# A two-layer diffusion-transformer block on one core: transposes of the attention weights, the place of four modulation parts, and the order of the mLSTM stage

## The chip, the core and the metric

The kernel runs on one core of one Trainium2 chip. TensorE multiplies matrices, VectorE and ScalarE do element-wise work, GpSimd (POOL in the profile) does element-wise work and issues DMAs from its own queue, SyncE (SP) issues DMAs. The metric is the device time of one execution in microseconds, as the median of several runs.

## The reference

All tensors are float32; the model width is 1024, the sequence 1024, the context 256. Each layer takes six modulation vectors from the condition, then a mixer and a mixture of experts with their residuals:

```python
def adaln(cond, w, b):
    m = jax.nn.silu(cond) @ w + b
    return jnp.split(m[..., None, :], 6, axis=-1)

for layer in range(2):
    sh1, sc1, gt1, sh2, sc2, gt2 = adaln(c, w_mod[layer], b_mod[layer])
    hx = modulate(x, norm_mix_g[layer], sh1, sc1)
    if layer == 0:   # mLSTM heads and sliding-window attention, both over ctx too
        hc = modulate(ctx, norm_mix_g[0], csh1, csc1)
        yx, _ = mixer_ab(hx, hc, ...)     # concat(mLSTM, attention) @ w_out
    else:
        yx = mixer_chunk_gmlp(hx, ...)
    x = x + gt1 * yx
    x = x + gt2 * ec_moe(modulate(x, norm_ffn_g[layer], sh2, sc2), ...)
return rmsnorm(x, final_norm_g)
```

The window attention has eight heads of 64. A block of 128 queries sees up to three blocks of 128 keys and all 256 context keys, with a sink added to the softmax's denominator. The mLSTM has four heads of 128 that run over eight chunks forward and backward. In `ec_moe` each of 16 experts takes its 128 best tokens.

## The kernel before

Matrix products are made of three products of rounded halves: high by high, low by high, high by low. `split` makes the halves of a weight: the high one on ScalarE (line 70), the low one on VectorE or GpSimd (line 71). A list scheduler decides the order of the instructions on each engine from the program, so the program's order is a wish. The stages, by the time of the profile:

- **First stage, 0 to 93 us** (`start`, `start_mod`, `heads_context`). x and ctx are loaded (tiles xt), normed and transposed; the first two modulation parts are computed from eight 1 MB loads wm that SyncE issues; the context's keys and values of the four mLSTM heads are projected, and their transposes stored.
- **Projections, 93 to 156 us** (`layer0_a`): keys, values, gates of the latent sequence. Line 298 is the matmul of every projection.
- **Attention, 156 to 596 us** (`attention`). Four pairs of heads c by eight query blocks n: 32 turns, each with two heads i. Scores S go to PSUM (two buffers in `pss`), ScalarE makes P = exp(S - max) and its row sums, VectorE the reciprocal of the denominator, `den`. Then each 128x128 tile of P is multiplied by a diagonal matrix `dg` = identity x den: this transposes and scales it at once (line 492, 304 tiles). The result is split to PH and PL and multiplied by the values. `fill(n)` hands out other work between those steps, 4, 2 and 3 steps a turn: the next heads' queries and the projections of the mLSTM heads. With every 28 of its steps come nine of `mods`.
- **mods** are ten of the twelve modulation parts (layer, w), in `mod_part`: eight steps of a 512 KB load wm on GpSimd's queue (line 667; `lm` holds two) and four matmuls of the weights against the 32-column condition (line 670), then the bias, and two transposes into `modc` or, for w = 2 and 5, a write to `s_gt`.
- **mLSTM and output projection, 596 to 825 us** (`lstm_main`, `lstm_finish`, `out_w`, `out_tile`, `layer0_b`). For each head and direction d: nP is the log-decay matrix and gets a mask (line 726), aq is multiplied by qT (line 732), kt is k transposed (line 718), wk and wc are k weighted by the state factors (lines 730, 728). The first head's element-wise work of that kind is on VectorE, that of the others on GpSimd. `out_w` loads w_out in 512 KB pieces and splits them, low halves on GpSimd.
- **Routing of the first layer, 825 to 850 us** (`route`): the router's scores lg are transposed, sorted on VectorE by a network of small operations, and the chosen tokens are gathered.
- **Experts, 850 to 1440 us** (`experts`), gMLP to 2078, second routing and experts to 2718. Expert weights come as 1 MB tiles mraw from SyncE into a ring (`moe_tile`), some ahead of the routing; tiles whose index is in `HELD` are held back and issued on GpSimd after the gather.

What line 492 does stands in these lines:

```python
dg = hp.tile([128, 128], F32, tag="dg", name="dg", bufs=2)
nc.vector.tensor_scalar(dg, self.ident, den, None, op0=ALU.mult)
...
nc.tensor.matmul(S[i][:, ...], P[:, j * 128:(j + 1) * 128], dg, start=True, stop=True)
```

## Time and profile before

| | |
|---|---|
| median of 3 runs | 2725.24 us (2724.99 to 2725.42) |
| the profiled execution | 2720.4 us, of which the span from first to last instruction is 2718.6 us |
| mean granted clock of TensorE in it | 0.968 |
| busy: TensorE, VectorE, ScalarE, GpSimd | 2529.9, 1879.9, 1511.4, 626.0 us |
| DMA | 644.02 MB, mean 237 GB/s |

A busy share is a mean over stages with different limits, so the share of a stretch is read beside it. Matmuls are pipelined: the duration of one instruction contains time in which the next already runs, and the distance from one start to the next is its price.

### The profile page before, as it was taken

Reading aid. Unit: us, or ns where it says so; the run is one execution under the profiler, and the core shown is the slowest. Engines: PE = TensorE matmul, PEld = TensorE weight load, DVE = VectorE, ACT = ScalarE, POOL = GpSimd, SP = SyncE. Lnnn points to the kernel's source line nnn. Section 1 sums busy time; section 2 is a strip of 40 time slices with the busy share of each in tenths; the row PEclk is TensorE's granted clock in tenths of the full one; section 3 lists DMA queues with packets and bytes.
Section 4 is the critical chain, followed back from the end, with each engine's and each line's share of the span. In section 5 each row is a group of like instructions: output and inputs, shape, how many; then the busy total and the mean of one; then the engine's idle time right before and its main releaser. Section 6 shows DMA issues by size and latency. Waiting matters only on the chain.

```text
span 2718.6 us, 35149 instructions
## 1 busy us (share of the span) xinstructions
PE 2529.9 (93%) x12847; PEld 2005.4 (74%) x12847; DVE 1879.9 (69%) x2830; ACT 1511.4 (56%) x2258; POOL 626.0 (23%) x413
## 2 busy tenths in 40 slices
PE   5999999998895999999998999999995999999996
PEld 3767777777774788888776887888884788888774
DVE  5566656567737999999885184116505899999887
ACT  4344344334424888888775223232322888888774
POOL 0010111115421222221102434533451021231001
PEclk8999999999996999999999999999997999999998
DMA  7344554457166999999966323342335999999995
GB/s 261 103 128 141 152 160 142 144 185 265 48 238 234 352 388 380 387 380 386 374 215 202 101 67 119 117 147 70 101 108 190 376 373 388 380 381 382 359 363 186
DMA packets 241642, 644.02 MB, mean 237 GB/s; under 512 B 18609, under 2 KB 85341, under 8 KB 240445
## 3 DMA queue, kind: packets, MB, share of 16 engines
q1 hardware_dynamic: 205136, 530.52, 52.3%
q0 software_dynamic: 25840, 89.99, 11.7%
q10 hardware_dynamic: 10492, 21.26, 2.3%
q8 instruction: 101, 1.65, 0.2%
q14 instruction: 73, 0.59, 0.1%
HBM read 589.06 MB, written 50.02 MB: 235 GB/s over the span
## 4 chain that ended last, share of the span: by engine, by line
PE 80%; DVE 8%; DMA 4%; issue 4%; ACT 3%; POOL 1%; POOLq 0%; ACTq 0%; SPq 0%; DVEq 0%
PE g L1134 13%; PE u L1134 13%; PE d L1134 12%; PE acc L298 8%; PE acc L1444 7%; PE acc L1518 6%; PE acc L1466 6%; PE S L492 2%; PE acc L805 2%; PE acc L670 2%; DMA wm<-in_w_mod_dram 1%; PE tr L1164 1%; DVE s2k L1460 1%; PE tr L1208 1%; PE O L501 1%
## 5 line engine op out<-in xcount | busy, mean ns | idle before, releaser
L71 DVE TENSOR_TENSOR ml<-mraw,mh 128x1024 fp32r<-128x1024 f32 x750 | 875.3, 1222 | 61.7 <-ACT mh L70 61.2
L70 ACT ACTIVATE mh<-mraw 128x1024 fp32r<-128x1024 f32 x750 | 769.3, 1064 | 138.6 <-PE g L1134 67.8
L71 POOL TENSOR_TENSOR wl<-wraw,wh 128x1024 fp32r<-128x1024 f32 (+1 forms) x132 | 253.6, 1930 | 349.8 <-ACT wh L70 349.8
L70 ACT ACTIVATE wh<-wraw 128x1024 fp32r<-128x1024 f32 (+1 forms) x163 | 143.0, 893 | 311.0 <-issue 123.6
L1232 POOL DMA_INDIRECT s_x<-xe,idx x28 | 66.9, 2388 | 655.0 <-ACT hidH L1210 394.4
L1134 PE MATMUL g<-mh,xH 128*128 128x512 f32 x512 | 206.4, 403 | 1.4 <-ACT xH L1169 1.4
L1134 PE MATMUL g<-ml,xH 128*128 128x512 f32 x512 | 205.3, 401 | 1.5 <-DVE ml L71 1.4
L1134 PE MATMUL g<-mh,xL 128*128 128x512 f32 x512 | 204.4, 399 | 0.0
L1134 PE MATMUL u<-ml,xH 128*128 128x512 f32 x512 | 203.4, 397 | 0.2
L1134 PE MATMUL u<-mh,xL 128*128 128x512 f32 x512 | 202.2, 395 | 0.0
L1134 PE MATMUL u<-mh,xH 128*128 128x512 f32 x512 | 202.2, 395 | 0.0
L1134 PE MATMUL d<-ml,hidH 128*128 128x512 f32 x496 | 197.5, 398 | 5.0 <-DVE ml L71 4.9
L1152 POOL DMA_INDIRECT xe<-s_xr,idx x32 | 137.7, 4303 | 270.7 <-ACT mh L70 131.0
L1134 PE MATMUL d<-mh,hidH 128*128 128x512 f32 x496 | 198.2, 400 | 1.6 <-DVE o L1229 1.6
L1134 PE MATMUL d<-mh,hidL 128*128 128x512 f32 x496 | 196.3, 396 | 0.0
L1444 PE MATMUL acc<-wh,h2k 128*128 128x512 f32 x512 | 163.7, 400 | 1.8 <-DVE h2k L1426 1.7
L1466 PE MATMUL acc<-h2k,wh 128*128 128x512 f32 x512 | 161.5, 396 | 0.0
L298 PE MATMUL acc<-hH,wh 128*128 128x512 f32 (+1 forms) x368 | 155.4, 422 | 1.6 <-DVE mrows L676 0.5
L1518 PE MATMUL acc<-wh,s2k 128*128 128x512 f32 x480 | 152.1, 397 | 0.0
L298 PE MATMUL acc<-hL,wh 128*128 128x512 f32 (+1 forms) x368 | 145.7, 396 | 0.0
L298 PE MATMUL acc<-hH,wl 128*128 128x512 f32 (+1 forms) x368 | 145.7, 396 | 0.0
L667 POOL DMA_DIRECT2D wm<-in_w_mod_dram x80 | 42.7, 534 | 406.6 <-PE acc L670 382.1
(469 smaller groups left out, 5238.9 us busy)
## 6 DMA issues: line engine op xcount, KB each, us to landing
mraw<-in_moe_w_down_dram SPq DMA_DIRECT2D x128, 1024.0 KB
mraw<-in_moe_w_gate_dram SPq DMA_DIRECT2D x126, 1024.0 KB
mraw<-in_moe_w_up_dram SPq DMA_DIRECT2D x124, 1024.0 KB
wm<-in_w_mod_dram POOLq DMA_DIRECT2D x80, 512.0 KB, 4.2
wraw<-in_gm_w_in_dram SPq DMA_DIRECT2D x64, 512.0 KB
wraw<-in_gm_w_out_dram SPq DMA_DIRECT2D x32, 512.0 KB
wraw<-in_ab_w_in_dram SPq DMA_DIRECT2D x30, 512.0 KB
wm<-in_w_mod_dram SPq DMA_DIRECT2D x8, 1024.0 KB
```

The lines of the kernel that those rows point to most:

```text
L70: nc.scalar.activation(h, src, AF.Copy)
L71: i = (nc.gpsimd if eng == "pool" else nc.vector).tensor_tensor(l, src, h.bitcast(F32), op=ALU.subtract)
L298: nc.tensor.matmul(acc, a[:, k, :], b[:, k, c0:c0 + n], start=(k == 0 and i == 0), stop=(k == KD - 1 and i == 2))
L492: nc.tensor.matmul(S[i][:, 512 - nl + j * 128:640 - nl + j * 128], P[:, j * 128:(j + 1) * 128], dg, start=True, stop=True)
L670: nc.tensor.matmul(acc[32 * j:32 * j + 32, :], lhs, wm[:, 256 * j:256 * (j + 1)], start=(k == 0), stop=(k == KD - 1))
L805: nc.tensor.matmul(acc, a[:, k, t * 128:(t + 1) * 128], b[:, k % 2, :], start=(k == 0 and i == 0), stop=(k == 3 and i == 2))
L1134: nc.tensor.matmul(acc[:, sl], a[:, k, :], b[:, sl], start=(k == 0 and i == 0), stop=(k == KD - 1 and i == 2))
L1152: f = nc.gpsimd.indirect_dma_start(out=xe, out_offset=None, in_=self.s_xr[layer], in_offset=bass.IndirectOffsetOnAxis(ap=self.idx[e], axis=0))
L1232: nc.gpsimd.indirect_dma_start(out=self.s_x[layer], out_offset=bass.IndirectOffsetOnAxis(ap=self.idx[e], axis=0), in_=o, in_offset=None, c ...
L1444: nc.tensor.matmul(acc[t], a[k][:, ts], b[:, k2, :], start=(k == 0 and i == 0), stop=(k == KD - 1 and i == 2))
L1466: nc.tensor.matmul(acc, a[:, k, :], b[k], start=(k == 0 and i == 0), stop=(k == KD - 1 and i == 2))
L1518: nc.tensor.matmul(acc, a[:, ts], b[k2], start=(c == 0 and i == 0), stop=(c == 15 and i == 2))
```

## The change

- `attention`: no dg. VectorE multiplies P by den in place, the whole 640 or 512 columns at once, after the first `fill`; then every tile is transposed through the identity.
- Four modulation parts leave the attention. Parts (0,2) and (0,3) go into the first stage: their wm tiles use the buffers of x's tiles, their loads stay on GpSimd's queue, and their sixteen steps are handed out in `heads_context`. Parts (1,3) and (1,4), called `HOLE`, are loaded as eight 1 MB tiles by SyncE into the ring of expert weights ahead of the output projection, and multiplied in the first layer's `route`, after the transpose of the scores, with ScalarE and GpSimd for what follows. The attention keeps six parts, one step of them with every fifth `fill` step.
- `lstm_main`: the mask additions and the products aq x qT are written ahead of the transposes of k.
- `out_w`: the low halves are made on VectorE.
- `HELD` is given for each layer; the first layer's is (18, 23), where the eight tiles of `HOLE` count in the index, and five tiles are held; the second keeps (11, 14).

```diff
                         yield
-            self.heads_context(late, pt, Ws, rows())
-    def heads_context(self, s, pt, Ws, more):
+            pm = self.pool(late, "pmod0", space=PSUM)
+            mods = itertools.chain(*(self.mod_part(xp, "xt", sm, pm, pt, 0, w) for w in (2, 3)))
+            self.heads_context(late, pt, Ws, rows(), mods)
+    def heads_context(self, s, pt, Ws, more, mods):
         nc = self.nc
...
             list(itertools.islice(more, 2))
+            list(itertools.islice(mods, (1, 1, 3, 3)[hd]))
             W = Ws.pop(0) if Ws else self.w_in(1024 + hd * 128)
...
             list(itertools.islice(more, 2))
+            list(itertools.islice(mods, (0, 2, 3, 3)[hd]))
         store(*kept)
-        for _ in more:
+        for _ in itertools.chain(more, mods):
             pass
...
                 nc.vector.reciprocal(den, den)
-                dg = hp.tile([128, 128], F32, tag="dg", name="dg", bufs=2)
-                nc.vector.tensor_scalar(dg, self.ident, den, None, op0=ALU.mult)
-                Ps.append((P, dg))
+                Ps.append((P, den))
             fill(self.FILLS[0])
...
                     fill(self.FILLS[1])
-                P, dg = Ps[i]
+                P, den = Ps[i]
+                nc.vector.tensor_scalar(P[:, 0:w], P[:, 0:w], den, None, op0=ALU.mult)
                 for j in range(nt):
-                    nc.tensor.matmul(S[i][:, 512 - nl + j * 128:640 - nl + j * 128], P[:, j * 128:(j + 1) * 128], dg, start=True, stop=True)
+                    nc.tensor.transpose(S[i][:, 512 - nl + j * 128:640 - nl + j * 128], P[:, j * 128:(j + 1) * 128], self.ident)
                 src = S[i][:, row].rearrange("p (j q) -> p j q", q=128)
...
             Qs = [Q, [], [], []]
-            mods = itertools.chain(*(self.mod_part(lm, pa, pt, i // 6, i % 6) for i in range(2, 12)))
+            mods = itertools.chain(*(self.mod_part(lm, "wm", lm, pa, pt, i // 6, i % 6) for i in range(4, 12) if (i // 6, i % 6) not in self.HOLE))
             work = itertools.chain(*(itertools.chain(self.query(pa, qp, c + 1, hx, Qs[c + 1]) if c < 3 else (),
...
                 for _ in itertools.islice(work, n):
-                    i = next(steps)
-                    if 9 * (i + 1) // 28 > 9 * i // 28:
+                    if next(steps) % 5 == 4:
                         next(mods, None)
...
                                         kh[base:base + 64, c0:c0 + n].bitcast(F32), op=ALU.subtract)
-    def mod_part(self, pool, pa, pt, layer, w):
-        nc, I = self.nc, self.I
+    def mod_step(self, acc, k, wm):
+        for j in range(4):
+            self.nc.tensor.matmul(acc[32 * j:32 * j + 32, :], self.silw[:, k].rearrange("p a s -> p (a s)"), wm[:, 256 * j:256 * (j + 1)],
+                                  start=(k == 0), stop=(k == KD - 1))
+    def mod_bias(self, pool, layer, w, bufs=1):
+        b = self.I["b_mod"]
+        bias = pool.tile([128, 256], F32, tag="mbias", name="mbias", bufs=bufs)
+        self.nc.gpsimd.dma_start(out=bias, in_=bass.AP(tensor=b.tensor, offset=b.offset + 6 * D * layer + D * w, ap=[[256, 4], [0, 32], [1, 256]]))
+        return bias
+    def mod_columns(self, rows, pt, layer, w, copy):
+        tr = pt.tile([128, 512], F32, tag="tr", name="tr")
+        for t in range(2):
+            self.nc.tensor.transpose(tr[:, t * 128:(t + 1) * 128], rows[:, t * 128:(t + 1) * 128], self.ident)
+        copy(self.modc[:, layer, 8 * w:8 * w + 8].rearrange("p (j t) -> p j t", t=2),
+             tr[:, 0:256].rearrange("p (t j r) -> p j t r", t=2, j=4)[:, :, :, 0])
+    def mod_part(self, wp, tag, pool, pa, pt, layer, w):
+        nc = self.nc
         acc = pa.tile([128, 512], F32, tag="acc", name="acc")[:, 0:256]
         for k in range(KD):
-            wm = pool.tile([128, D], F32, tag="wm", name="wm")
-            nc.gpsimd.dma_start(out=wm, in_=I["w_mod"][layer, k * 128:(k + 1) * 128, D * w:D * (w + 1)])
-            lhs = self.silw[:, k].rearrange("p a s -> p (a s)")
-            for j in range(4):
-                nc.tensor.matmul(acc[32 * j:32 * j + 32, :], lhs, wm[:, 256 * j:256 * (j + 1)], start=(k == 0), stop=(k == KD - 1))
+            wm = wp.tile([128, D], F32, tag=tag, name="wm")
+            nc.gpsimd.dma_start(out=wm, in_=self.I["w_mod"][layer, k * 128:(k + 1) * 128, D * w:D * (w + 1)])
+            self.mod_step(acc, k, wm)
             yield
+        bias = self.mod_bias(pool, layer, w)
         rows = pool.tile([128, 256], F32, tag="mrows", name="mrows", bufs=1)
-        bias = pool.tile([128, 256], F32, tag="mbias", name="mbias", bufs=1)
-        b = I["b_mod"]
-        nc.gpsimd.dma_start(out=bias, in_=bass.AP(tensor=b.tensor, offset=b.offset + 6 * D * layer + D * w, ap=[[256, 4], [0, 32], [1, 256]]))
         nc.vector.tensor_tensor(rows, acc, bias, op=ALU.add)
...
         else:
-            tr = pt.tile([128, 512], F32, tag="tr", name="tr")
-            for t in range(2):
-                nc.tensor.transpose(tr[:, t * 128:(t + 1) * 128], rows[:, t * 128:(t + 1) * 128], self.ident)
-            nc.vector.tensor_copy(self.modc[:, layer, 8 * w:8 * w + 8].rearrange("p (j t) -> p j t", t=2),
-                                  tr[:, 0:256].rearrange("p (t j r) -> p j t r", t=2, j=4)[:, :, :, 0])
+            self.mod_columns(rows, pt, layer, w, nc.vector.tensor_copy)
         yield
+    HOLE = ((1, 3), (1, 4))
+    def hole_load(self):
+        self.hole = []
+        for layer, w in self.HOLE:
+            for kp in range(4):
+                raw = self.moe_tile()
+                self.nc.sync.dma_start(out=raw, in_=self.I["w_mod"][layer, 256 * kp:256 * (kp + 1), D * w:D * (w + 1)].rearrange("(k p) c -> p k c", p=128))
+                self.hole.append(raw)
+    def hole_mods(self, p, ps, pt):
+        for i, (layer, w) in enumerate(self.HOLE):
+            acc = ps.tile([128, 512], F32, tag="mod", name="mod")[:, 0:256]
+            for k in range(KD):
+                self.mod_step(acc, k, self.hole[4 * i + k // 2][:, k % 2, :])
+            rows = p.tile([128, 256], F32, tag="mrows", name="mrows", bufs=2)
+            self.nc.scalar.activation(rows, acc, AF.Copy)
+            self.mod_columns(rows, pt, layer, w, lambda o, x: self.nc.scalar.activation(o, x, AF.Copy))
+            m = self.modc[:, layer, 8 * w:8 * w + 8]
+            self.nc.gpsimd.tensor_tensor(m, m, self.bcols[:, 48 * layer + 8 * w:48 * layer + 8 * w + 8], op=ALU.add)
     def lstm_main(self, lp, hd):
...
         nc.sync.dma_start(out=og, in_=self.s_o[hd])
+        eng = nc.gpsimd if hd else nc.vector
+        for d in range(2):
+            mask = self.maskb if d else self.maskf
+            eng.tensor_tensor(nP[d], nP[d], mask[:, None, :].to_broadcast([128, NT, 128]), op=ALU.add)
+        for d in range(2):
+            nc.vector.tensor_tensor(aq[d], aq[d], qT, op=ALU.mult)
         kt = lp.tile([128, NT, 128], F32, tag="kt", name="kt")
...
             nc.tensor.matmul(S[:, c * 128:(c + 1) * 128], kT[:, c * 128:(c + 1) * 128], qT[:, c * 128:(c + 1) * 128], start=True, stop=True)
-        eng = nc.gpsimd if hd else nc.vector
         for d in range(2):
-            mask = self.maskb if d else self.maskf
-            eng.tensor_tensor(nP[d], nP[d], mask[:, None, :].to_broadcast([128, NT, 128]), op=ALU.add)
             wc.append(lp.tile([128, 2, 128], F32, tag="wc", name="wc", bufs=2))
...
         for d in range(2):
-            nc.vector.tensor_tensor(aq[d], aq[d], qT, op=ALU.mult)
             u = self.psn.tile([128, 130], F32, tag="num", name="num")
...
             Ws.append(self.load_w(self.I["ab_w_out"][0, r0:r0 + 256, 512 * cb:512 * (cb + 1)].rearrange("(k p) c -> p k c", p=128), [128, 2, 512],
-                                  dma=self.nc.gpsimd))
+                                  "dve", dma=self.nc.gpsimd))
         return Ws
...
             self.moe_open(self.m0, 0, 8)
+            self.hole_load()
             lp = self.pool(s, "lp2")
...
         tr = pp.tile([128, 512], F32, tag="tr", name="tr")
-        nc.tensor.transpose(tr[:, 0:128], lg.rearrange("p t e -> p (t e)"), self.ident)
+        last = nc.tensor.transpose(tr[:, 0:128], lg.rearrange("p t e -> p (t e)"), self.ident)
         rows = p.tile([128, 128], F32, tag="rows", name="rows")
...
                     nc.vector.match_replace(work[:, h:h + 64], s1[:, h + 8 * r:h + 8 * r + 8], work[:, h:h + 64], -1.0)
+        if layer == 0:
+            with self.tc.issue_after(last.ins):
+                self.hole_mods(p, self.hole_ps, self.hole_pt)
         def stages(src, dst, n, sizes):
...
     def moe_raw(self, name, layer, e, kp):
-        held = self.HELD[0] <= self.mrawi < self.HELD[1]
+        h0, h1 = self.HELD[layer]
+        held = h0 <= self.mrawi < h1
         raw = self.moe_tile()
...
         return raw
-    HELD = (11, 14)
+    HELD = ((18, 23), (11, 14))
     def moe_w(self, name, layer, e, k, low=True):
...
                 pp = self.pool(r, "rpp0", bufs=3, space=PSUM)
+                self.hole_ps = self.pool(r, "rmod", bufs=2, space=PSUM)
+                self.hole_pt = self.pool(r, "rmpt", bufs=2, space=PSUM)
                 self.route(rw, pp, 0)
```

VectorE in the attention, around the two heads of one turn; ast holds the maxima, sums and den, mx and PL belong to the turns before. Before:

```order
L477 TENSOR_TENSOR ast<-ast 128x1
L473 SCALAR_TENSOR_TENSOR ast<-ast,nsink 128x1
L478 RECIPROCAL ast<-ast 128x1
L480 TENSOR_SCALAR dg<-cst,ast 128x128
L508 TENSOR_TENSOR mx<-O,mx 64x256
L477 TENSOR_TENSOR ast<-ast 128x1
L478 RECIPROCAL ast<-ast 128x1
L480 TENSOR_SCALAR dg<-cst,ast 128x128
L495 TENSOR_TENSOR PL<-S,PH 128x5x128 x2
```

After:

```order
L481 TENSOR_TENSOR ast<-ast 128x1
L477 SCALAR_TENSOR_TENSOR ast<-ast,nsink 128x1
L482 RECIPROCAL ast<-ast 128x1
L493 TENSOR_SCALAR P<-P,ast 128x640
L71 TENSOR_TENSOR wl<-wraw,wh 128x1024
L481 TENSOR_TENSOR ast<-ast 128x1
L482 RECIPROCAL ast<-ast 128x1
L493 TENSOR_SCALAR P<-P,ast 128x640
L498 TENSOR_TENSOR PL<-S,PH 128x5x128 x2
```

The diagonal was made right behind the reciprocal; now the scaling of P stands there. In the rows of after, the low half of a weight (wl) stands between the two heads' chains.

TensorE in the first stage, around the last transposes of the context's keys and values (kcT, vcT); xt is x, cH and cL are the context's halves. Before:

```order
L228 MATMUL tr<-cst,kcT 128x128
L229 MATMUL tr<-cst,vcT 128x128
L228 MATMUL tr<-cst,kcT 128x128
L229 MATMUL tr<-cst,vcT 128x128
L213 MATMUL tr<-cst,xt 128x128 x8
L228 MATMUL tr<-cst,kcT 128x128
L229 MATMUL tr<-cst,vcT 128x128
L228 MATMUL tr<-cst,kcT 128x128
L229 MATMUL tr<-cst,vcT 128x128
L298 MATMUL acc<-cH,wh 128x256
L298 MATMUL acc<-cL,wh 128x256
L298 MATMUL acc<-cH,wl 128x256
```

After:

```order
L230 MATMUL tr<-cst,kcT 128x128
L231 MATMUL tr<-cst,vcT 128x128
L230 MATMUL tr<-cst,kcT 128x128
L231 MATMUL tr<-cst,vcT 128x128
L213 MATMUL tr<-cst,xt 128x128 x8
L665 MATMUL acc<-wm,silw 32x256 x16
L230 MATMUL tr<-cst,kcT 128x128
L231 MATMUL tr<-cst,vcT 128x128
L230 MATMUL tr<-cst,kcT 128x128
L231 MATMUL tr<-cst,vcT 128x128
L677 MATMUL tr<-cst,mrows 128x128 x2
L302 MATMUL acc<-cH,wh 128x256
```

Sixteen of the 64 matmuls L665 (four of the sixteen steps; in the profile each is two instructions) stand between the transposes of x and those of the last head, and the two transposes of a finished part ahead of the projections that follow; the other 48 stand further up.

GpSimd at the start of the mLSTM stage, with the halves and loads of w_out (wl, wraw) and the second head's nP and wc. Before:

```order
L71 TENSOR_TENSOR wl<-wraw,wh 128x1024 x2
L78 DMA wraw<-in_ab_w_out_dram 128x2x512 x2
L71 TENSOR_TENSOR wl<-wraw,wh 128x1024
L728 TENSOR_TENSOR wc<-kctx,colG 128x256 x2
L78 DMA wraw<-in_ab_w_out_dram 128x2x512
L726 TENSOR_TENSOR nP<-nP,cst 128x1024 x2
```

After:

```order
L78 DMA wraw<-in_ab_w_out_dram 128x2x512 x2
L767 TENSOR_TENSOR wc<-kctx,colG 128x256 x2
L753 TENSOR_TENSOR nP<-nP,cst 128x1024 x2
L78 DMA wraw<-in_ab_w_out_dram 128x2x512
L769 TENSOR_TENSOR wk<-kt,colG 128x1024
```

The low halves that stood ahead of the second head's wc and nP are no longer in GpSimd's queue.

## Rows read from the trace of the kernel before

**Rows 1.** The page, part 1: busy us and share of the span by engine.

```profile
PE 2529.9 (93%) x12847; PEld 2005.4 (74%) x12847; DVE 1879.9 (69%) x2830; ACT 1511.4 (56%) x2258; POOL 626.0 (23%) x413
```

**Rows 2.** Busy time by stretch: stretch, length, engines' busy us, granted clock, DMA share, GB/s.

```profile
20.00:50.00 30.00, 19.01 (x112) 11.28 (x112) 12.66 (x40) 12.88 (x26) 0.00 (x0) 0.77 1.01 349
50.00:100.00 50.00, 38.52 (x268) 35.20 (x269) 44.34 (x91) 31.20 (x55) 0.34 (x2) 0.86 0.39 109
200.00:600.00 400.00, 395.25 (x2583) 301.99 (x2582) 237.57 (x508) 156.35 (x326) 46.79 (x86) 1.00 0.49 153
600.00:750.00 150.00, 121.57 (x700) 103.71 (x699) 115.63 (x212) 73.94 (x251) 79.49 (x62) 0.91 0.45 161
830.00:843.00 13.00, 0.00 (x0) 0.00 (x0) 12.14 (x82) 5.85 (x7) 1.45 (x3) 0.50 0.56 205
900.00:1400.00 500.00, 497.37 (x2325) 400.72 (x2324) 467.93 (x476) 419.24 (x517) 98.92 (x26) 1.00 1.01 376
```

**Rows 3.** Timeline of TensorE: start, us, operation, count, idle time before and its releaser.

```profile
843.27 0.60 PE L1017 MATMUL tr<-sort,cst 32*16 32x128 f32 x2 [14.88 <-DVE sort L1003]
```

**Rows 4.** Groups of instructions by shape, TensorE, 156 to 600 us.

```profile
L492 PE MATMUL S<-dg,P 128*128 128x128 f32 x608 | 81.2, 280 | 2.3 <-DVE ast L477 1.7 <-DVE dg L480 0.6
L670 PE MATMUL acc<-wm,silw 128*32 128x256 f32 x624 | 56.6, 391 | 1.9 <-DMA wm<-in_w_mod_dram 1.8
```

**Rows 5.** Timeline of TensorE from 305 us.

```profile
305.48 0.40 PE L298 MATMUL acc<-hH,wl 128*128 128x512 f32 x1
305.80 0.64 PE L670 MATMUL acc<-wm,silw 128*32 128x256 f32 x8
306.37 0.50 PE L298 MATMUL acc<-hH,wh 128*128 128x512 f32 x1
306.71 0.40 PE L298 MATMUL acc<-hL,wh 128*128 128x512 f32 x1
306.94 0.39 PE L298 MATMUL acc<-hH,wl 128*128 128x512 f32 x1
...
309.20 1.38 PE L492 MATMUL S<-dg,P 128*128 128x128 f32 x10
310.34 0.48 PE L298 MATMUL acc<-hH,wh 128*128 128x512 f32 x1
```

**Rows 6.** Timeline of TensorE from 664 us, the transposes of kT.

```profile
664.30 0.60 PE L718 MATMUL tr<-cst,kT 128*128 128x128 f32 x4
664.74 1.28 PE L722 MATMUL S<-qT,kT 128*128 128x128 f32 x10
```

**Rows 7.** Groups of instructions by shape, VectorE, 156 to 600 us.

```profile
L71 DVE TENSOR_TENSOR wl<-wraw,wh 128x1024 fp32r<-128x1024 f32 x16 | 19.5, 1221 | 6.4 <-ACT wh L70 6.2
L480 DVE TENSOR_SCALAR dg<-cst,ast 128x128 f32<-128x128 f32 x64 | 18.1, 286 | 3.8 <-issue 2.3
...
L312 DVE TENSOR_SCALAR hx<-pad,convw 128x1024 f32<-128x1024 f32 x8 | 6.0, 753 | 0.0
```

**Rows 8.** The chain that ended last, first stage: start, us, what.

```profile
24.40 9.38 DMA wm<-in_w_mod_dram
```

**Rows 9.** One tile, wm, 156 to 600 us.

```profile
DMA to landing us min/median/max: 3.8/4.2/7.5
```

**Rows 10.** Groups of instructions by shape, GpSimd, 590 to 860 us.

```profile
L71 POOL TENSOR_TENSOR wl<-wraw,wh 128x1024 fp32r<-128x1024 f32 x8 | 19.4, 2428 | 22.1 <-ACT wh L70 22.1
```

**Rows 11.** The chain that ended last, mLSTM stage.

```profile
607.13 5.07 POOL wl L71 x2
...
776.65 2.40 POOL wl L71
```

**Rows 12.** Groups of instructions by shape, VectorE, 590 to 800 us.

```profile
L732 DVE TENSOR_TENSOR aq<-aq,qT 128x1024 f32<-128x1024 f32 x8 | 13.4, 1697 | 0.0
```

**Rows 13.** Timeline of VectorE from 305 us.

```profile
307.30 0.16 DVE L477 TENSOR_TENSOR ast<-ast 128x1 f32<-128x1 f32 x1 [1.07 <-ACT ast L476]
...
312.67 0.15 DVE L477 TENSOR_TENSOR ast<-ast 128x1 f32<-128x1 f32 x1
```

## The prediction

> **What bounds the kernel now.** I read the busy shares first: TensorE works 93% of the span and VectorE 69% [rows 1], so work taken off TensorE counts wherever TensorE is not waiting. Then the stretches. In the attention (200 to 600 us) TensorE is busy 395.25 of 400 us at full clock and VectorE 237.57, so TensorE alone sets the pace and every 100 ns taken from it there is time [rows 2]. The first stage is different: between 50 and 100 us TensorE idles 11.5 us while VectorE is busy 44.34 of 50, and from 20 to 50 us the DMA engines are full (1.01) [rows 2]. In the mLSTM stage (600 to 750) TensorE idles 28.4 of 150 us, with VectorE at 115.63 and GpSimd at 79.49 [rows 2]. While the first layer's routing sorts, TensorE does nothing for 14.88 us [rows 3]. So the change touches one stage where TensorE's work is the time and three where it moves work into gaps.
>
> **Attention: plain transposes.** The diagonal matmul is recorded 608 times at 280 ns, two instructions for each of 304 tiles [rows 4]. Instructions overlap, so I use the pace: ten start at 309.20 and what follows starts at 310.34, which is 0.108 us an instruction with the step into another shape left in [rows 5]. A transpose through the identity is one instruction: four of kT start at 664.30 and the next matmul at 664.74, 0.11 us each [rows 6]. So 304 tiles go from two instructions to one: 304 x 0.108 = −32.8 us. The Trainium skill ("Perfetto Trace Analysis", section on optimizing Tensor performance) says that logical transposes should use the transpose and not a standard matmul; [rows 5, 6] agree and give the factor as two.
>
> **Attention: four of ten modulation parts leave.** One step of a part is eight instructions. From 305.48 to 306.71 stand one L298 matmul, one step and another L298; L298 alone paces at 0.23 (306.71 to 306.94), so the step costs 1.23 − 0.46 = 0.77 us, of which 0.57 is the eight instructions and 0.2 the change of shape [rows 5]. A part has eight steps, 6.2 us; four parts −24.6 us (−18 at 0.57). Both together −57 us if TensorE stays busy.
>
> **Attention: what VectorE gets.** The diagonal (128x128, 286 ns, 64 times, 18.1 us) goes. Scaling a whole P of 640 or 512 columns is not in the trace; it lies between 286 ns for 128 columns and 753 ns for 1024 by the same operation [rows 7]. On the line between these, 0.55 and 0.49 us, 64 times some 34 us: VectorE gains 16 us and goes from 59% to about (237.6 + 15) / 350 = 72%. Nothing is charged as throughput, since it stays below TensorE. As delay it counts: the scale stands between the reciprocal and the transposes, 0.26 us longer than the diagonal did, behind in-order work such as a 1.22 us low half. If none of it were covered, 64 x 0.26 = 17 us; if the matmuls given out between scores and transposes cover all, nothing. They now hold fewer modulation steps, so I take +8. Attention: −57 + 8 = −49 (−58 to −34).
>
> **First stage.** Two parts bring 16 steps: 12.4 us of TensorE work at 0.77. By the order they stand ahead of the last context transposes and of the stage's last projections. TensorE has 11.5 us of idle time there, so the floor is nothing; the ceiling is all 12.4 us plus the DMA time. Of the loads, 1 MB needs no modulation result and comes free early, just as the 1 MB loads that the first modulation waits for (9.38 us from 24.40 on) fill the DMA engines [rows 8, 2]: at 349 GB/s that is up to 3 us. Later loads reuse a tile only after TensorE has read it, 4.2 us to landing each [rows 9]. I take +5 (0 to +15): most lands in waits for VectorE, some steps arrive late and hold what is behind them.
>
> **mLSTM stage.** Eight low halves leave GpSimd, 19.4 us at 2428 ns; two of them stand in the chain for 5.07 us at 607 and one for 2.40 at 776 [rows 10, 11]. On VectorE the same operation takes 1221 ns [rows 7]: +9.8 us on an engine at 77%. While GpSimd works, VectorE's own operations stretch (aq mean 1697 ns against the 1221 of an undisturbed one of that size) [rows 12, 7]; 8 x 0.48 = 3.8 us of that may come back. Giving masks and queries out earlier moves little: the scheduler leaves the first head's order as it was, and the mask additions of the second now follow the context weights directly instead of three low halves. Gain at most 7.5 + 3.8 + some waits behind GpSimd, −14; loss, if the extra VectorE work lands on the chain where the low halves did not, +3. I take −6. The Trainium skill ("SBUF — State Buffer", "Who interferes with whom") says that VectorE and GpSimd lock each other out of a shared port, which fits aq's 1697 ns; by itself it would return all 3.8 us and change nothing in the sum.
>
> **First routing.** Sixty-four matmuls (128 of the profile's instructions) and four transposes go between the transpose of the router's scores and the first matmul after the sort, a gap of 14.88 us at clock 0.50 [rows 3, 2]. At full clock they take 128 x 0.0714 = 9.1 us (0.57 for eight [rows 5]), at half clock about 18. The clock must first rise, so I put their end 12 to 17 us after their start, nearer the half clock's 18 than 9: level with the sort, cost 0 to 3 us. Their eight 1 MB tiles take the place of expert weights, which then load only once TensorE has read those tiles: 8 MB at the experts' 376 GB/s is 22.3 us, begun about when the sort begins, and the gather of the first tokens may meet the end of it. In the experts DMA share is 1.01 while TensorE is busy 497.37 of 500 us [rows 2], so a late tile is made up only slowly. I take +2 (0 to +8) for both.
>
> **Sum.** −49 + 5 − 6 + 2 = −48. The profiled execution took 2720.4 us (span 2718.6); the median of the runs is 4.8 above it, 2725.24. 2720.4 − 48 + 4.8 = 2677.2, so 2677 us.
>
> **Rivals.**
> - *VectorE becomes the attention's limit.* With 72% busy in order and two score buffers, TensorE waits for P in most of the 64 turns. For it: an addition for the second head's denominator, at 312.67, comes 5.4 us after the first head's, at 307.30, behind other work on VectorE [rows 13]. Against it: TensorE hardly waited in spite of that. If a turn lost 0.4 us more than the 0.13 I charge, 64 x 0.4 = +25: 2702.
> - *The transposes cost what the pair cost.* A transpose of f32 may run at half the rate of the instruction it replaces. Against it: 0.11 us each for kT [rows 6]. Then −32.8 falls away: 2710.
> - *A transpose costs a quarter of the pair.* The kT row shows a half, but for four in a row. Then 304 x (0.216 − 0.054) = −49 in place of −32.8: 2661. The Trainium skill ("TensorE: Matmul & The Clock Gate", Terms) gives a transpose mode "4× faster for FP32"; [rows 5, 6] speak for two.
> - *First stage in full.* +15 in place of +5: 2687.
> - *Slower: the modulation's loads starve.* The six parts left in attention load through GpSimd's queue, two tiles deep. Today a load lands in 4.2 us and TensorE waits 1.8 us in all for 76 of them [rows 9, 4]. Steps will come about every 350 / 48 = 7.3 us, so a tile has some 14 us. If scaling P held these loads up until they took x us, TensorE would lose 48 (x − 14); from x = 15 the gain of 48 us is gone, at 16 the time is 2725 + 48 = 2773. The rest of VectorE's work is as dense today and leaves landings at 4.2. The Trainium skill ("SBUF — State Buffer", the trap that VectorE blocks DMA) says that descriptor writing by GpSimd starves while VectorE runs in a two-port mode, as a scaling does; the 4.2 us beside a VectorE that is 59% busy shows no such thing at this density.
>
> **How the numbers follow.** A difference under 0.2% (5.4 us) can't be told from none here. Forecast 0.63; VectorE's limit 0.15; transposes dear 0.05; transposes at a quarter 0.05; first stage in full 0.08; starving or anything else that eats the gain 0.04, split between the same and slower. Faster 0.96, same 0.02, slower 0.02. The forecast's own bounds: attention and the other three seldom all err one way, so 2662 to 2692. The range goes to the quarter-price transposes below, 2659, and to VectorE's limit above, 2702; outside lie the dear transposes, the starved loads and what lies past the bounds.
>
> **What the new profile should show.** L495 transposes 304 times at a pace near 0.11 us; TensorE 97% busy or more in the attention, which ends some 45 us earlier relative to its start; the P scale at 0.5 to 0.6 us; no wait on wm worth naming. First projections of layer0_a start about 5 us later. No GpSimd low halves and VectorE's aq nearer 1.2 us. The 128 matmul instructions done by the sort's end, the first expert no more than 5 us later after the scores' transpose. Wrong would be: TensorE idle over 20 us in the attention, a first stage longer by over 10 us, or experts waiting on weights.

## The result and the profile after

The changed kernel takes 2700.93 us (median of three runs, 2698.77 to 2703.46) against 2725.24: ratio 0.9911, 95% interval 0.9889 to 0.9934. That is 24.3 us faster, half of the 48 that were forecast. The profiled execution's span is 2697.0 us, 21.6 less than before.

The page's busy shares ([rows 1] before) and the stretches ([rows 2]; the attention now lies between 172 and 546 us, the mLSTM stage from 546, the sort from 791):

```profile
PE 2499.4 (93%) x12543; PEld 1973.6 (73%) x12543; DVE 1892.9 (70%) x2834; ACT 1507.3 (56%) x2262; POOL 588.2 (22%) x391
```

```profile
20.00:50.00 30.00, 20.63 (x113) 10.99 (x106) 11.63 (x30) 10.63 (x22) 1.11 (x2) 0.66 1.02 367
50.00:100.00 50.00, 42.27 (x349) 31.72 (x352) 38.96 (x86) 28.11 (x48) 9.27 (x18) 0.97 0.76 235
200.00:540.00 340.00, 333.09 (x2011) 254.41 (x2012) 253.36 (x508) 157.89 (x330) 28.80 (x50) 1.00 0.37 118
546.00:791.00 245.00, 208.61 (x1171) 175.51 (x1169) 152.70 (x304) 94.84 (x286) 76.48 (x70) 0.91 0.51 181
791.00:815.00 24.00, 10.92 (x134) 5.26 (x134) 13.66 (x92) 9.03 (x13) 3.31 (x7) 0.71 0.98 380
```

TensorE is still 98% busy in the attention, VectorE 75%. DMA between 50 and 100 us went from 109 to 235 GB/s, and TensorE idles 13 us of the 24 from 791 on.

To see where time came and went, I take four instructions that mark the stages, from the views of one line (count, ns, first to last start): the first scores, the last product with the values, the transpose of the router's scores, the matmul after the sort.

```profile
L466 PE MATMUL S<-amask,identb x64: 281/336/337, 172.7 to 537.6; 128*128 128x384 bf16 x48, 128*128 128x256 bf16 x16
L504 PE MATMUL O<-PH,vst x152: 276/281/388, 192.5 to 545.9; 128*128 128x256 f32 x152
L1012 PE MATMUL tr<-cst,lg x2: 472/474/476, 791.0 to 2053.5; 128*128 128x128 f32 x2
L1059 PE MATMUL tr<-sort,cst x4: 388/404/416, 815.3 to 2069.4; 32*16 32x128 f32 x4
```

Before, the same marks stood at 156.2, 583.7, 827.9 and 843.3. Their distances in us, with the forecast terms:

| stretch | before | after | difference | forecast |
|---|---|---|---|---|
| to the first scores (first stage, projections) | 156.2 | 172.7 | +16.5 | +5 |
| attention, to the last product with the values | 427.5 | 373.2 | −54.3 | −49 |
| mLSTM, to the scores' transpose | 244.2 | 245.1 | +0.9 | −6 |
| sort, to the matmul after it | 15.4 | 24.3 | +8.9 | +2 |
| all that follows | 1875.3 | 1881.7 | +6.4 | 0 |

The prediction's +2 was for the sort and for expert weights that load later, so part of it belongs to the last row. The attention gained what was forecast and a little more. Three stages where work was to vanish in gaps, and what follows them, took back more than half of it.

### The profile page after: what moved, and what is told of

Same layout as the page of the kernel before. It is cut to its first block, busy times and chain, and to the rows that moved or that the text cites. A ratio compares the mean times of both kernels' runs of the same rounds, so it can differ in the third digit from the quotient of the medians.

```text
span 2697.0 us, 34507 instructions
## 1 busy us (share of the span) xinstructions
PE 2499.4 (93%) x12543; PEld 1973.6 (73%) x12543; DVE 1892.9 (70%) x2834; ACT 1507.3 (56%) x2262; POOL 588.2 (22%) x391
## 4 chain that ended last, share of the span: by engine, by line
PE 79%; DVE 9%; DMA 5%; issue 3%; ACT 3%; POOL 1%; POOLq 0%; ACTq 0%; DVEq 0%; SPq 0%
PE g L1177 13%; PE u L1177 13%; PE d L1177 12%; PE acc L302 8%; PE acc L1487 7%; PE acc L1561 6%; PE acc L1509 6%; PE acc L843 2%; PE S L495 1%; DMA wraw<-in_ab_w_in_dram 1%; PE acc L665 1%; PE tr L1207 1%; PE tr L1251 1%; PE O L504 1%; DVE s2k L1503 1%
## 5 line engine op out<-in xcount | busy, mean ns | idle before, releaser
L71 POOL TENSOR_TENSOR wl<-wraw,wh 128x1024 fp32r<-128x1024 f32 (+1 forms) x124 | 238.6, 1933 | 324.1 <-ACT wh L70 324.1
L1195 POOL DMA_INDIRECT xe<-s_xr,idx x32 | 143.1, 4473 | 265.1 <-ACT mh L70 121.7
L1275 POOL DMA_INDIRECT s_x<-xe,idx x28 | 45.1, 1612 | 681.4 <-ACT hidH L1253 446.8
L688 POOL DMA_DIRECT2D wm<-in_w_mod_dram x64 | 34.6, 543 | 441.8 <-PE acc L665 392.3
```

The costliest lines, as they stand in the source:

```text
L71: i = (nc.gpsimd if eng == "pool" else nc.vector).tensor_tensor(l, src, h.bitcast(F32), op=ALU.subtract)
L688: nc.gpsimd.dma_start(out=wm, in_=self.I["w_mod"][layer, k * 128:(k + 1) * 128, D * w:D * (w + 1)])
L1195: f = nc.gpsimd.indirect_dma_start(out=xe, out_offset=None, in_=self.s_xr[layer], in_offset=bass.IndirectOffsetOnAxis(ap=self.idx[e], axis=0))
L1275: nc.gpsimd.indirect_dma_start(out=self.s_x[layer], out_offset=bass.IndirectOffsetOnAxis(ap=self.idx[e], axis=0), in_=o, in_offset=None, c ...
```

## The experiments

Rows are from the profile of the kernel named ahead of them; times are medians, beside runs of the kernel before on the same chip (2723.2 us for e1 to e4, 2724.5 for e5, e6, e7 and e10, 2723.1 for e8, e9 and e11). Experiments 3 and 5 leave loads out; they were run once, for the stretches alone.

A stretch comes from one trace of a kernel, and it varies where the kernel does not. The first scores start between 155.3 and 156.6 us in the five kernels with the first stage as before, and between 168.3 and 175.5 in the six with the changed one. The mLSTM stretch is 241.5 to 245.9 us in the three kernels where it is as before, and 242.4 to 246.1 in the five where it is as in the changed kernel.

**1 (e1). Why the sort is late.** In the changed kernel VectorE's timeline shows the first maximum of the sort behind the matmuls of the two parts, with which it shares no data:

```profile
791.53 0.29 DVE L1015 COPY rows<-tr 128x128 f32<-128x128 f32 x1 [0.57 <-PE tr L1012]
791.86 0.23 DVE L1016 COPY work<-rows 128x128 f32<-128x128 f32 x1
801.03 0.35 DVE L1032 MAX8 sort<-work 128x8 f32<-128x64 f32 x2 [8.95 <-PE mod L665]
```

The matmuls read silw, whose pool closes with the first half of the kernel; the sort's tiles are allocated after that. The edit keeps silw in a pool that closes after the routing:

```diff
+            hs = es.enter_context(ExitStack())
+            sp = self.pool(hs, "silw")
...
-                self.silw = mc.tile([128, KD, 16, 2], F32, name="silw")
+                self.silw = sp.tile([128, KD, 16, 2], F32, name="silw")
...
                 self.route(rw, pp, 0)
+            hs.close()
```

> The changed kernel with the condition tile silw in a pool of its own that stays open until the routing's end; nothing else differs. In the changed kernel the first maximum of the sort stood 8.95 us behind the last matmul of the two parts that are multiplied in the routing. Theory: the sort's result tile lies on memory that silw gave back when the pools of the first half closed, and so waits for silw's last reader. Then the sort starts right behind the copy of the scores, the distance from the scores' transpose to the matmul after the sort goes from 24.3 back to about 15.5 us, and the time falls by 8 to 9 us, to about 2692. Rival: the sort is held by the matmuls or the loads themselves; then the distance stays over 22 us and the time within 2 us of 2701.

```profile
791.47 0.29 DVE L1015 COPY rows<-tr 128x128 f32<-128x128 f32 x1 [0.57 <-PE tr L1012]
791.79 0.23 DVE L1016 COPY work<-rows 128x128 f32<-128x128 f32 x1
792.05 0.35 DVE L1032 MAX8 sort<-work 128x8 f32<-128x64 f32 x2
```

The wait is gone, the sort takes 16.4 us from mark to mark, and the time is 2693.1 us (ratio to before 0.9883, 0.9863 to 0.9904). The matmuls themselves fit: they run from 791.4 to 801.8 us beside the sort. Theory held: the sort waited for memory, not for data. The other four kernels with silw kept show 16.1 to 16.5 us as well, about 1 more than the 15.4 of before.

**2 (e2). The transposes alone**, in the kernel before (the same three edits in `attention`, nothing else).

> The kernel before with the plain transposes and the scaling of P alone; modulation parts, mLSTM and routing as before. Theory: a transpose is half the pair, 304 x 0.108 = 33 us less TensorE work, some of it lost to waits for the scaling: the attention (first scores to last product with the values, 427.5 us before) 25 to 33 us shorter, 2692 to 2700. Rival, transposes as dear as the pair: within 3 us of 2725. Rival, a quarter of the pair: 45 us or more less, below 2681. Rival, VectorE becomes the limit: 10 to 15 us less, about 2712.

2706.5 us (0.9942, 0.9916 to 0.9969); the attention fell by 15.0 us to 412.5. That misses the theory's 25 to 33 and is about what the VectorE rival had given. The transposes are not the reason: from start to start they take 34.4 us where the pairs took 66.7 (sums over the timeline). TensorE waits, and mostly not for VectorE, as its waits and two short stretches show:

```profile
PE acc L669 <- DMA wm<-in_w_mod_dram: 9.7, 9, 1.7
PE S L491 <- DVE ast L477: 1.8, 1, 1.8
```

```profile
178.40:181.80 3.40, 3.40 (x15) 3.31 (x15) 1.32 (x3) 0.66 (x1) 1.82 (x3) 0.50 0.51 151
533.40:540.20 6.80, 5.41 (x19) 2.92 (x19) 0.82 (x1) 0.70 (x1) 0.53 (x1) 0.50 0.52 161
```

TensorE waits 9.7 us for modulation weights (1.8 before, [rows 4]) and 3.4 us for the scaling and the denominator. The granted clock falls to 0.50 (1.2 GHz) in two stretches: one begins 0.8 us after a wait of 1.7 us for wm, the other after waits of 0.9 and 1.0 us that ended at 531.02 and 532.69; a wait of 1.4 us lies inside it. The kernel before has one such stretch in its attention, behind a wait of 1.7 us for the denominator:

```profile
497.00:500.20 3.20, 3.20 (x14) 2.81 (x13) 0.74 (x1) 0.70 (x1) 0.00 (x0) 0.50 0.22 86
```

**3 (e10). The same with one load a part** (`if k == 0:` ahead of the tile and its load in `mod_part`).

> The kernel of e2 (plain transposes alone) with one load of modulation weights for each part in place of eight, all eight steps multiplying that tile: 70 of 80 loads are left out, and ten modulation vectors are not those of the reference. Theory: with shorter transposes the steps come before their loads, two tiles deep, and TensorE waits 9.7 us for them; without the loads the attention falls from 412.5 to 400 to 404 us. Rival, the scaling on VectorE holds TensorE: 409 us or more.

The attention takes 389.3 us, 23 less than in experiment 2 and 11 below the theory's 400 to 404, with VectorE's work unchanged; TensorE waits for the scaling 0.5 us, and the clock stays at 1.00:

```profile
156.00:546.00 390.00, 385.54 (x2437) 284.17 (x2433) 276.11 (x585) 172.03 (x362) 14.92 (x23) 1.00 0.22 68
```

So the loads, two tiles deep, held the transposes' gain back: 7.9 us more of waits in the open than before, some 3 of half clock (10.2 us at half speed against 3.4 before), the rest in smaller delays that the views do not name one by one. VectorE is not the limit. Not all of the 23 us is the transposes' gain: against the kernel before, 38.2 us are gone and the transposes are worth 33, so some 5 us are what the loads cost there already; the kernel before was not run with few loads.

**4 (e3). Parts (0,2) and (0,3) back in the attention.**

```diff
-            mods = itertools.chain(*(self.mod_part(xp, "xt", sm, pm, pt, 0, w) for w in (2, 3)))
+            mods = itertools.chain(*(self.mod_part(xp, "xt", sm, pm, pt, 0, w) for w in ()))
...
-                    if next(steps) % 5 == 4:
+                    if next(steps) % 4 == 3:
```

with `range(2, 12)` for `range(4, 12)` in `layer0_a`.

> The changed kernel with parts (0,2) and (0,3) back in the attention, one step of a part with every fourth fill step; the first stage is that of before. Theory: their loads and steps cost the first stage 16.5 us (first scores at 172.7 against 156.2), in the attention they cost 16 x 0.77 = 12.4: first scores at 156 to 158, the attention 12 us longer, the time 2 to 5 us less, about 2697. Rival, they cost the same in both places, as TensorE work alone: within 2 us of 2701. Rival, the attention has room for them: 10 us less or more.

2699.8 us (0.9915, 0.9889 to 0.9941), the same within the scatter. The first scores are back at 156.1, 16.6 us earlier, but the attention is 20.4 us longer, not 12.4: TensorE waits 5.7 us for wm and 6.9 for the scaling and the denominator, and the clock's mean is 0.98. Experiment 11 says the same.

**5 (e4). One load in the first stage** (its sixteen steps multiply one tile):

```diff
-            wm = wp.tile([128, D], F32, tag=tag, name="wm")
-            nc.gpsimd.dma_start(...)
-            self.mod_step(acc, k, wm)
+            if tag != "xt" or not k % 8 and w == 2:
+                wm = wp.tile([128, D], F32, tag=tag, name="wm")
+                nc.gpsimd.dma_start(...)
+                self.wm1 = wm
+            self.mod_step(acc, k, self.wm1)
```

> The changed kernel, but in the first stage one 512 KB tile of modulation weights is loaded and all sixteen steps multiply it; 15 of the 16 loads are left out, so parts (0,2) and (0,3) are not those of the reference. Theory: the loads take the DMA engines from the projections' weights and so make the stage late; then the first scores start at 158 to 164 in place of 172.7. Rival: TensorE's sixteen steps and their place in its order make it late; then at 170 or later.

First scores at 162.5, on the theory's side: 10.2 of the 16.5 us belong to the loads, 6.3 to the steps, their order and the first load. With the spread named above the loads' share is 6 to 13 us. The chain of the changed kernel's first stage shows how. Before, it held a single such row, 3.77 us long; with one load it holds two, 5.33 and 4.86:

```profile
60.22 5.86 DMA wraw<-in_ab_w_in_dram
...
74.35 9.47 DMA wraw<-in_ab_w_in_dram
...
88.85 7.83 DMA wraw<-in_ab_w_in_dram
...
99.05 3.38 DMA wraw<-in_ab_w_in_dram
```

wraw are the projections' weights. Between 70 and 100 us the DMA share is 0.89 in the changed kernel and 0.38 with one load.

**6 (e7). Two loads in flight instead of up to ten**, on the kernel of experiment 1 (`wp = self.pool(late, "wm0", bufs=2, side="right")` in place of x's tiles).

> The kernel of e1 (silw kept, 2693) with a ring of two tiles of their own for the first stage's modulation loads, in place of the ten tiles of x. Theory: the stage is late because six loads at a time (3 MB) fill the DMA engines just when the projections' weights are due; with two in flight the weights land earlier, the first scores come at 164 to 169 in place of 173.4, the time 2685 to 2689. Rival, TensorE's order decides: each step then waits for its own load behind the last one, the first scores at 173 or later, the time 2693 or more.

2697.0 us (0.9906, 0.9885 to 0.9926), not clear of experiment 1, and the first scores at 178.2, where the theory had 164 to 169: the rival's side. In the chain most rows of the projections' weights give way to the modulation's own:

```profile
57.63 4.77 DMA wm<-in_w_mod_dram
...
68.47 4.89 DMA wraw<-in_ab_w_in_dram
...
88.13 5.07 DMA wm<-in_w_mod_dram
...
105.10 6.13 DMA wm<-in_w_mod_dram
```

So my theory that fewer loads in flight would cure the stage falls. With many tiles the loads hold up other weights; with two, what stands behind a late step in TensorE's order waits with it. The second half of this is read from the chain and not tested by itself.

**7 (e5). Low halves of w_out back on GpSimd** (without `"dve"`), **8 (e6). masks and queries as before** (the moved lines of `lstm_main` put back).

> The changed kernel with the low halves of w_out back on GpSimd. From the last product with the values to the transpose of the router's scores the changed kernel took 245.1 us, before 244.2. Theory: what GpSimd loses VectorE pays, so this part is worth nothing: the stretch 242 to 248 us, the time within 3 us of 2701. Rival, the prediction's step: it gave some 6 us and something else took them; then the stretch is 249 us or more, the time about 2707.

> The changed kernel with the mask additions and the products aq x qT behind the transposes of k, as before. Theory: the order written makes no difference, since the scheduler places them: the same stretch 242 to 248 us, the time within 3 us of 2701. Rival, giving them out early puts them ahead of what TensorE waits for and cost the gain of the low halves: the stretch 240 us or less, the time about 2695.

Without the low halves on VectorE the mLSTM stretch is 240.3 us and the time 2695.3 (0.9897, 0.9879 to 0.9916), better than the changed kernel, which neither theory had. Without the order of `lstm_main` it is 242.0 us and 2700.3 (0.9909, 0.9891 to 0.9927): no difference that counts. The waits of the changed kernel in this stage told why (TensorE, 546 to 791 us), beside the issues on SyncE and ScalarE:

```profile
PE tr L935 <- DMA wr<-in_moe_w_router_dram: 7.7, 1, 7.7
PE num L787 <- DVE nP L782: 6.7, 3, 3.6
```

```profile
702.00 17.51 SPq L709 DMA_DIRECT2D mraw<-in_w_mod_dram  x8
```

```profile
702.71 0.41 ACTq L929 DMA_DIRECT2D wr<-in_moe_w_router_dram  x1
```

The router's weights wr (64 KB) are issued 0.7 us behind the first of eight 1 MB loads, and TensorE waits 7.7 us for them. Before, wr was issued at 745.57 and the first of the 1 MB loads at 746.24, and the wait was 1.5 us. In experiment 7 the order is again that of before, though the edit does not touch it, and TensorE does not wait for wr at all:

```profile
702.44 0.39 ACTq L929 DMA_DIRECT2D wr<-in_moe_w_router_dram  x1
703.09 11.56 SPq L709 DMA_DIRECT2D mraw<-in_w_mod_dram  x8
```

So what experiment 7 gained is the wait for wr; it does not say that the low halves on VectorE cost anything.

**9 (e8). Router's weights first**, on the kernel of experiment 1 (the load on ScalarE's queue goes):

```diff
+            wr = rt.tile([128, KD, 16], F32, tag="wr", name="wr")
+            nc.sync.dma_start(out=wr, in_=I["moe_w_router"][0].rearrange("(k p) e -> p k e", p=128))
             self.hole_load()
```

> The kernel of e1 (silw kept, 2693) with the load of the router's weights wr on SyncE's queue ahead of the eight tiles of the two parts, in place of ScalarE's queue beside them. In the changed kernel TensorE waited 7.7 us for wr (5.1 in e1), before 1.5. Theory: the eight 1 MB loads were issued first and wr queued behind them, and that ate what the mLSTM stage had won. Then the wait for wr is gone, the stretch from the last product with the values to the scores' transpose 245 to 238 to 241 us, the time 2687 to 2689. Rival: the wait only moves to the loads of w_out or x behind it; then the stretch stays over 243.

```profile
692.27 0.38 SPq L906 DMA_DIRECT2D wr<-in_moe_w_router_dram  x1
706.76 8.22 SPq L709 DMA_DIRECT2D mraw<-in_w_mod_dram  x8
```

The wait is gone, the mLSTM stretch 236.7 us, below the theory's 238 to 241, the time 2686.2 (0.9861, 0.9841 to 0.9881): the lowest median of the kernels that load everything. Experiment 11, with the same stage, has 237.4; the five kernels with the late wr have 242.4 to 246.1.

**10 (e9). The same with the low halves on GpSimd.**

> The kernel of e8 with the low halves of w_out on GpSimd. If the low halves on VectorE are worth something, the stretch is longer than that of e8, by up to 6 us as predicted. If they are worth nothing, it is within 2 us of e8 (238 to 243), and the gain of e5 over the changed kernel was the wait for wr alone.

mLSTM stretch 241.3 us, 2691.2 (0.9878, 0.9862 to 0.9895). With wr out of the way the low halves on VectorE are worth 4.6 us by these two traces. Experiments 7 and 11 are a second pair without a wait for wr, 240.3 and 237.4, which gives 2.9. The times' intervals overlap, so the sign rests on four traces and the size is some 3 to 5 us.

**11 (e11). Experiment 9 with eight parts in the attention.**

> The kernel of e8 with parts (0,2) and (0,3) back in the attention, as in e3. e3 had the first scores 16.6 us earlier and the attention 20.4 us longer than the changed kernel, with 5.7 us of waits for the loads and three dips of the clock. If that is how it is, 2 to 5 us more than e8; if the dips were chance, 4 us less than e8.

2686.9 us (0.986, 0.9844 to 0.9877), the same as experiment 9: first scores at 156.6, 18.9 us earlier, attention 390.9, 18.7 us longer, with 9.5 us of waits for wm. Neither of the two expectations came: where the two parts stand makes no difference that these runs show.

## Why the prediction was right, and where not

The time lies inside the stated range, 2659 to 2702, but only 1 us below its top, and 9 us above the forecast's own bounds of 2662 to 2692. The top was set by the rival in which VectorE limits the attention, and that did not happen: TensorE waits 1.1 us for the scaling in all, and without most loads the attention falls on (experiment 3). So that the range held is luck. Against the forecast the stretches gave −5.3 us in the attention, +11.5 in the first stage, +6.9 each in the mLSTM stage and the sort, and +6.4 behind.

**What bounds the kernel** held: the attention's time is TensorE's.

**Plain transposes**: right, and the size too. Five start at 306.17 and the next matmul at 306.69, 0.104 us each:

```profile
306.17 0.77 PE L495 MATMUL S<-cst,P 128*128 128x128 f32 x5
306.69 0.47 PE L302 MATMUL acc<-hH,wh 128*128 128x512 f32 x1
```

From 66.7 to 33.9 us in all, −32.8 as worked out. The recorded 0.108 us does not come from its own rows (1.14 us for ten is 0.114 [rows 5]); over the whole attention the pair's instructions take 0.110 us and the transposes 0.112, and the slips cancel. The rivals of a transpose at the pair's price or a quarter of it are out: the factor is two. The Trainium skill ("TensorE: Matmul & The Clock Gate", Terms) has 4× for its transpose mode, without saying against what; the measured 2× decides for this plain f32 transpose.

**Four parts out**: right. Modulation matmuls go from 53.4 to 38.7 us from start to start, and the projections' 840 matmuls from 217.0 to 209.2, which fits the prediction's 0.2 us for each change of shape (32 steps, 6.4 us): −22.5 for the −24.6 worked out.

**What VectorE gets**: the scale is 553 ns, 0.55 as estimated, and VectorE is 73% busy over the attention (172 to 546 us) for 72; the +8 of delay was too much. In the changed kernel's attention TensorE idles 9.3 us in all against 5.3, and waits 1.1 us for the scale:

```profile
L495 PE MATMUL S<-cst,P 128*128 128x128 f32 x304 | 43.8, 276 | 3.8 <-DVE ast L481 2.5 <-DVE P L493 1.1
L665 PE MATMUL acc<-wm,silw 128*32 128x256 f32 x368 | 36.9, 390 | 2.5 <-DMA wm<-in_w_mod_dram 2.5
```

```profile
L493 DVE TENSOR_SCALAR P<-P,ast 128x640 f32<-128x640 f32 x48 | 26.2, 553 | 1.0
```

What the prediction did not see is that the two halves of the attention's change need each other: alone the transposes give 15 of their 33 us (experiment 2), mostly because the ten parts' loads then come too late (experiment 3).

**First stage**: mis-sized, +16.5 for +5 and outside its bounds of 0 to +15. The step that failed is the price of the DMA: it counted 3 us for the two early loads and gave the other 14 (7 MB) only their own 4.2 us to landing, with no cost to other loads. They meet the projections' weights (experiment 5: 10.2 us). More than 10 us here was one of the prediction's own signs of being wrong.

**mLSTM stage**: the mechanism was right and its gain lost to a new wait. The low halves give some 3 to 5 us (experiment 10), 6 were forecast; the wait for wr, 7.7 us for 1.5, took them (experiments 7 to 9). The prediction had wr in none of its rows. The order of masks and queries is worth nothing, as said. What comes back to VectorE was put in the wrong place: aq fell from 1697 to 1538 ns only, 1.3 us of the 3.8, and with the low halves back on GpSimd (experiment 7) it is 1592, so even that is not shown to be theirs. But other work of VectorE shortened, the low halves mL and lL of what goes into the output projection, here before and after:

```profile
L71 DVE TENSOR_TENSOR mL<-attl,mH 128x512 fp32r<-128x512 f32 x8 | 9.2, 1162 | 3.0 <-ACT mH L70 2.9
L71 DVE TENSOR_TENSOR lL<-og,lH 128x1024 fp32r<-128x1024 f32 x4 | 8.1, 2068 | 1.8 <-ACT lH L70 1.8
```

```profile
L71 DVE TENSOR_TENSOR mL<-attl,mH 128x512 fp32r<-128x512 f32 x8 | 5.8, 755 | 0.0
L71 DVE TENSOR_TENSOR lL<-og,lH 128x1024 fp32r<-128x1024 f32 x4 | 4.6, 1220 | 0.0
```

That is 6.7 us by the means, and in experiment 7 they are back at 1154 and 2064 ns. Against it one product of og went from 3.2 to 9.4 us. In sum VectorE took over 9.8 us of low halves and is busy 152.7 us in the stage for 152.5 before.

**First routing**: the step failed. What cost 8.9 us is a wait of the sort for silw's memory, which I had not looked for; without it the sort takes 16.4 us for 15.4, inside the 0 to 3 that were forecast (experiment 1). The matmuls were priced too high. They took 9.5 us, not 12 to 17, though the clock was 0.50 for the first half of them:

```profile
791.40:796.40 5.00, 5.00 (x49) 2.33 (x52) 0.52 (x2) 5.00 (x6) 0.39 (x1) 0.50 0.91 360
796.40:800.90 4.50, 4.50 (x85) 2.30 (x77) 0.00 (x0) 1.89 (x3) 0.00 (x0) 1.00 1.01 341
```

In a row of 128 four start every 0.43 us at the low clock and every 0.215 at the full one, 0.054 each where the prediction had 0.0714 from a single step of eight [rows 5].

**Starved loads**: no sign. In the changed kernel's attention a load lands in 4.3 us at the median, with VectorE 73% busy, a tenth of the time in the scaling. Where TensorE did wait for loads (experiment 2), they landed in 4.1: they were due sooner, not slower.

**What follows**: +6.4 us from the sort to the end. 3.3 of them arise in the second half of the first layer's experts. They are no chance: from the middle of the experts' matmuls to nine tenths of them it takes 231.8 us in all three kernels with the routing as before (before, experiments 2 and 3) and 235.0 to 235.5 in all ten with the two parts in it. TensorE waits there for low halves of expert weights (ml), 2.4 us in the changed kernel for 1.0 before, with the DMA share at 1.00. This fits the late expert weights of which the prediction spoke, and experts waiting for weights were one of its signs of being wrong; no run varied these loads, so the cause is argued and not shown. The other 3 us lie within what executions differ: experiment 2, with nothing changed behind the attention, has +4.1 over the whole stretch.

Sum: 16.5 − 54.3 + 0.9 + 8.9 + 6.4 = −21.6, the spans' difference.

## What to carry to other kernels

Work moved into a gap brings its loads and its memory along: look for which other load is due in the gap, and in which queue order, and whether a tile that lives longer now sits under buffers that the gap's own work writes. A false wait shows as a releaser that shares no data with the waiter; here it cost 8 us, and the router's weights behind eight large loads 6 (7.7 us of waiting for 1.5). Where two cuts hit the same stage, price them together: shortening the matmuls around a two-deep ring of loads uncovers the loads.

## What was not expected of the hardware

In an attention where TensorE is 96% busy, waits of 0.9 to 1.7 us were followed by 3.4 and 6.8 us at a granted clock of 0.50 (experiment 2), and the kernel before has 3.4 us behind a wait of 1.7. The length of a single wait does not decide it: the changed kernel's attention has waits of 2.1 and 1.7 us, experiment 3 one of 1.5, and both stay at 1.00. A load of 64 KB in 64-byte rows, issued 0.7 us after the first of eight 1 MB loads, was there for TensorE only at 719.2 us, 16.5 us after its issue at 702.71; issued 0.65 us ahead of them (experiment 7), it was there after 11.9 us at the latest, without a wait.
